# Two more chunk pairs of a projection as block products, and the recurrence's chunks ahead of them

## The chip, the core and the metric

The kernel runs on one core of a Trainium2 chip. The metric is device time in microseconds (us): the median of three runs. The core has a matrix engine (TensorE, PE in the profile; PEld is its loading of weights), a vector engine (VectorE, DVE), an engine for functions of one operand (ScalarE, ACT), GpSimd (POOL) and SyncE (SP). The last two issue transfers here: SyncE loads and stores, GpSimd transfers that add to what stands at their destination.

## The reference

One layer for x of 1024 positions by 1024 channels, all in float32:

```python
h = rms_norm(x, g_mix)
z = h @ w_in + b_in                       # 1024 -> 8 groups of columns
va, ga, xb, gb, sa, sb = split(z)         # 1024, 1024, 1536, 1536, 1024, 1024
u = conv31(va * sigmoid(ga))              # causal, per channel, 31 taps
y_a = silu(layer_norm(u)) @ w_a_out
v = rg_lru(conv4(xb))                     # 16 heads' gates, then a scan over positions
y_b = (v * gelu(gb)) @ w_b_out
x = x + (sigmoid(sa) * y_a + sigmoid(sb) * y_b) @ w_o
x = x + relu(rms_norm(x, g_mlp) @ w_1) ** 2 @ w_2
out = rms_norm(x, g_final)
```

The layer norm's mean and variance run over the 1024 channels of a position, so they need all eight convolutions.

## The kernel before

Positions are kept as two halves of 512, the even and the odd ones. A float32 operand is split into a high part that the fast matmul format holds and a low rest, and a product is three matmuls: high by high, high by low, low by high. One matmul is 128 by 128 weights against 512 positions.

The columns of w_in are taken in chunks of 128. VA and GA have 8 chunks each (j = 0 to 7), XB 12, GB 12, SA 8, SB 8.

*Part 1* (the loop over `s`, `chunk_mm`, L735) takes a chunk directly: 48 matmuls (8 blocks of 128 channels, 3 products, 2 halves). In before these are 28 chunks: all of XB, VA and GA, in the order of the list `CH`. Each chunk's weights are loaded (win_raw), written by ScalarE rounded and negated into the place of the low part (L66: win_l) and rounded into the high part (L68: win_h), and a GpSimd transfer adds the exact weights to the negated ones, so that the rest is left (L67). Behind a pair VA, GA, `u_out` forms u = va * sigmoid(ga): ScalarE at L587, VectorE at L453, a helper that records many of VectorE's operations. Between the chunks stand the gates of the recurrence: 16 heads (`head_mm`, L530 to L532), placed by the table `HS0`; behind every four heads (one group) come exponentials and roots on ScalarE (L556, L557, L564) and three scans on VectorE (`scan_tile`, L573 to L576, one for each of 12 tiles of 128 channels; its result is stored to hd). A scan is placed `lag` chunks late.

*Part 2* (the list `zseq`, `z_mm`, L933) takes two chunks together. Their weights are a matrix of 2 by 2 blocks (512 channels by 128 columns) and x is one of 2 by 2 blocks (512 channels by 512 positions). Seven products of blocks give the result that eight would (Strassen's way, in Winograd's form), of 12 matmuls each: 84 for a pair instead of 96. Product 1 and 2 and 4 use blocks of weights as they are; 3, 5, 6 and 7 use sums of blocks, made by VectorE (`z_sums`: zs). Each product's weights are split like the others (`z_lhs`: zo, from zw or zs), with the rest by a GpSimd transfer (L67), or for products 5 and 7 by ScalarE (L776) and VectorE (L453). Likewise products 4 to 7 use sums of x's blocks (`x_load` loads them as xs, `x_sum` adds, four per half of the positions, and `x_parts` splits them into xs4h, xs4l to xs7h, xs7l). A pair's weights are loaded by `z_load` in two halves (zw), in order of the table `ZL`. The results are put together out of the banks z..a to z..u by `z_out`. In before part 2 has 14 pairs: GB 6, SA 4, SB 4.

The convolutions (`conv`, L639 to L655) are VectorE's filling: eight of 49 operations, mostly taps (L648), which `vector_work` puts wherever VectorE would have to wait for TensorE by the planner's clocks (`at` adds an operation's assumed cost to an engine's clock; `later` holds an operation back until its operands are ready). `vector_work(inf)` in stage b takes whatever is left. Conv j's result is stored to yd[j] (L656), and `sum_up` has GpSimd add it into one tile ysum (L607, L609), with a transfer that accumulates.

*Stage b* multiplies by w_b_out (`b_mm`, L1121: eight steps j of 72 matmuls, banks yb). Its operand, the products of the scans and the gates, comes back from memory (hgd to hg) and is split: ScalarE (hgh, L1023), VectorE (hgl), twelve tiles, the last one behind stage b's first matmuls. Its weights are split by ScalarE (L1099) and VectorE (L1085). During step j = 1 the sum of the convolutions is split too (`n_parts`: ysumh by ScalarE, L1159; ysuml by VectorE), and at j = 2, behind 32 matmuls, `n_mean` places the four matmuls that give the mean (mu, L1149, L1150). The convolutions are loaded back as q by 16 loads (L1142), and the variance follows at j = 4. Behind that come the rest of the layer norm, w_a_out, w_o and the two products of the MLP, which the change leaves alone.

The order on each engine is the order in which the program states the operations (a manual schedule); nothing is reordered later. What the planner's clocks decide is only where VectorE's operations stand.

## Time and profile before

| | us |
|---|---|
| median of three runs | 1548.71 (1548.26 to 1549.64) |
| profiled execution | 1549.04 |
| its span | 1547.2 |
| PE, DVE, ACT, POOL busy | 1535.6, 1214.5, 903.6, 188.6 |
| part 2 begins (first matmul of z0a) | 360.57 |
| stage b begins (first matmul of yb) | 623.05 |
| mean's first matmul (mu) | 668.72 |

The lines of the profile read as: line of the kernel, engine, operation, written tile <- read tiles, shape, count, busy time, mean of one in ns, idle time before it and what ended that. In a timeline the first two numbers are start and duration in us, and in square brackets stand the idle time before it and its releaser. In a table of windows each engine has its busy us and its number of instructions, then the granted clock of TensorE (1.00 is full), the share of time in which the DMA engines were busy, and GB/s. Matmuls overlap by a little, so their durations (0.39) are longer than the spacing of their starts.

### The profile page before, as it was taken

How to read it: one execution, taken by the hardware profiler on the slowest of the kernel's cores; microseconds unless marked ns; L12 is line 12 of the kernel's file. 1: busy time of each engine (PE TensorE's matmuls, PEld its weight loads, DVE VectorE, ACT ScalarE, POOL GpSimd, SP SyncE). 2: the span in 40 equal slices, each digit the busy share in tenths (PEclk: the TensorE clock that was granted, in tenths of full speed). 3: DMA queues.
4: the chain of work that ended last, by engine and by line, in shares of the span. 5: the costliest groups of instructions: out<-in, count | busy, mean ns of one | idle time of the engine just before them, and what ended most of it. 6: DMA issues, size and time to landing. Idle time of an engine off the chain costs nothing. (4 is left out here: it accounts for less than half of the span.)

```text
span 1547.2 us, 19086 instructions
## 1 busy us (share of the span) xinstructions
PE 1535.6 (99%) x6804; PEld 1264.6 (82%) x6804; DVE 1214.5 (78%) x1641; ACT 903.6 (58%) x1266; POOL 188.6 (12%) x226
## 2 busy tenths in 40 slices
PE   9999999999999999999999999999999999999998
PEld 7878888788888888888888887888888888888886
DVE  6999989999899983468568868765555558888897
ACT  6748677576667667435375777545444475555553
POOL 0000000002222222000022322000000001111110
PEclk9999999999999999999999999999999999999999
DMA  8653554678999889854579978523333779888852
GB/s 348 169 127 95 160 140 134 158 227 214 264 267 256 195 206 259 270 196 126 185 195 306 194 171 198 211 75 124 113 115 111 242 216 229 226 223 223 205 124 109
DMA packets 124943, 294.18 MB, mean 190 GB/s; under 512 B 12464, under 2 KB 30512, under 8 KB 124848
## 3 DMA queue, kind: packets, MB, share of 16 engines
q1 hardware_dynamic: 93312, 213.00, 40.7%
q0 software_dynamic: 31392, 79.71, 28.1%
q8 instruction: 53, 0.87, 0.2%
q14 instruction: 42, 0.34, 0.1%
q10 hardware_dynamic: 144, 0.26, 0.1%
HBM read 152.93 MB, written 58.72 MB: 137 GB/s over the span
## 5 line engine op out<-in xcount | busy, mean ns | idle before, releaser
L735 PE MATMUL z<-xh,win_h 128*128 128x512 f32 x400 | 125.0, 390 | 0.0
L735 PE MATMUL z<-xl,win_h 128*128 128x512 f32 x400 | 123.5, 390 | 0.0
L1873 DVE TENSOR_TENSOR acc<-acc,d 128x1024 f32<-128x1024 f32 x72 | 87.8, 1220 | 33.4 <-PE d L1861 32.7
L735 PE MATMUL z<-xh,win_l 128*128 128x512 f32 x400 | 99.4, 391 | 0.0
L735 PEld LDWEIGHTS z<-xh,win_l 128*128 128x128 f32 x400 | 75.2, 188 | 16.8
L735 PEld LDWEIGHTS z<-xh,win_h 128*128 128x128 f32 x400 | 75.1, 188 | 16.5 <-ACT win_h L68 0.4
L648 DVE SCALAR_TENSOR_TENSOR y<-u,vec,y 128x511 f32<-128x511 f32 (+14 forms) x120 | 88.5, 737 | 0.0
L735 PEld LDWEIGHTS z<-xl,win_h 128*128 128x128 f32 x400 | 75.1, 188 | 15.8
L648 DVE SCALAR_TENSOR_TENSOR yt<-u,vec,yt 128x511 f32<-128x511 f32 (+6 forms) x112 | 82.6, 737 | 0.0
L648 DVE SCALAR_TENSOR_TENSOR y<-yt,csum,y 128x511 f32<-128x511 f32 (+6 forms) x112 | 82.6, 737 | 0.0
L542 ACT ACTIVATE g<-rg,vec 96x1024 f32<-96x1024 f32 x32 | 35.6, 1113 | 79.6 <-PE rg L532 79.6
L1540 ACT ACTIVATE o<-s 128x512 fp32r<-128x512 f32 x58 | 34.7, 623 | 52.8 <-DVE s L1525 31.3
L67 POOL DMA_DIRECT2D win_l<-win_raw x25 | 21.6, 865 | 319.1 <-ACT win_l L66 248.4
L476 DVE SCALAR_TENSOR_TENSOR v<-xb,vec,v 128x1023 f32<-128x1023 f32 (+2 forms) x36 | 46.2, 1282 | 11.4 <-ACT v L467 10.4
L67 POOL DMA_DIRECT2D zo<-zw x42 | 36.2, 862 | 133.6 <-ACT zo L66 125.3
L1121 PE MATMUL yb<-hgl,wb_h 128*128 128x512 f32 x168 | 51.8, 390 | 0.0
L1121 PE MATMUL yb<-hgh,wb_h 128*128 128x512 f32 x168 | 51.8, 389 | 0.0
L66 ACT ACTIVATE zo<-zw 128x512 fp32r<-128x512 f32 x42 | 26.3, 626 | 30.7 <-DMA zw<-in_w_in_dram 8.7
L67 POOL DMA_DIRECT2D db_1l<-wr x7 | 6.0, 860 | 309.8 <-DMA wr<-in_w_dram 254.0
L1121 PE MATMUL yb<-hgh,wb_l 128*128 128x512 f32 x168 | 41.0, 390 | 0.0
L1085 DVE TENSOR_TENSOR o<-s,o 128x512 fp32r<-128x512 f32 x58 | 38.8, 682 | 0.0
L1121 PEld LDWEIGHTS yb<-hgh,wb_h 128*128 128x128 f32 x168 | 31.6, 188 | 6.5
(1795 smaller groups left out, 4672.9 us busy)
## 6 DMA issues: line engine op xcount, KB each, us to landing
w_raw<-in_w_dram SPq DMA_DIRECT2D x36, 512.0 KB, 5.5
fr<-fd SPq DMA_DIRECT2D x32, 512.0 KB, 5.9
wr<-in_w_dram SPq DMA_DIRECT2D x32, 512.0 KB, 6.5
zw<-in_w_in_dram SPq DMA_DIRECT2D x28, 512.0 KB, 5.9
win_raw<-in_w_in_dram SPq DMA_DIRECT2D x25, 512.0 KB, 4.1
win_l<-win_raw POOLq DMA_DIRECT2D x25, 512.0 KB, 4.5
zo<-zw POOLq DMA_DIRECT2D x42, 256.0 KB, 5.6
gates<-zg SPq DMA_DIRECT2D x32, 256.0 KB, 4.0
```

The costliest lines, as they stand in the source:

```text
L66: nc.scalar.activation(l, src, AF.Copy, scale=-1.0)
L67: nc.gpsimd.dma_start(l, src, accum_op=ALU.add)
L476: nc.vector.scalar_tensor_tensor(v[:, d:S], a[:, 0:S - d], cbw_c[:, w * 12 + t:w * 12 + t + 1], v[:, d:S], ALU.mult, ALU.add)
L542: nc.scalar.activation(a, gps.pop((n, gi))[:HD, :], AF.Sigmoid, bias=(ba_c, bx_c)[gi][:, n:n + 1])
L648: nc.vector.scalar_tensor_tensor(o[:, k:], a[:, 0:HS - k], c, o[:, k:], ALU.mult, add)
L735: nc.tensor.matmul(zps[s][:, HALVES[hf]], w[:, k, :], xw[k][part][hf], start=n == 0, stop=n == 23)
L1085: tt(l, src, h.bitcast(F32), ALU.subtract)
L1121: nc.tensor.matmul(ps[hf], a, b[:, HALVES[hf]], start=n == 0, stop=n == len(todo) - 1)
L1540: nc.scalar.activation(o[:, 0], src, AF.Copy)
L1873: tt(acc[p, q2], acc[p, q2], ps, ALU.add)
```

## The change

VA and GA of j = 6 and 7 leave part 1 and become the first two pairs of part 2, which are now 16; a pair is VA j with GA j, and the new `z_branch` forms u out of the quadrants as they come. Part 1 has 24 chunks, in a new order: XB's chunks stand ahead of the VA, GA pair that they stood behind, and the heads follow (`HS0`). `lag` is 0 for all groups; tile 10's scan moves from part 1 to the start of part 2 (`ZX` slot 0), tile 11's from slot 7 to slot 2. `x_load` stands at the chunks 4 and 2 from the end, in place of 5 and 3, and several `x_parts` move into part 2.

In part 2 the first eight products are 1 and 2 of pairs 0 and 1 and then of pairs 2 and 3, with the rest of pairs 0 and 1 behind. The blocks that products 1 and 2 of pairs 2 and 3 need are loaded on their own (`z_first`: zf, four loads of 256 KB, before part 2), and their full loads come later as for the others. The loop over `z_sums` ahead of part 2 is gone; all are made within the loop. Of the four dummy matmuls that opened a bank (`z_bank`) one is left.

```diff
--- before.py
+++ after.py
@@ -668,7 +668,7 @@
 
     def x_load(c2):
 
-        xq[c2] = {n: ep.tile([P, S], F32, tag="e", name=f"xs{n}_{c2}") if (n, c2) == (21, 0) else T(f"xs{n}_{c2}")
+        xq[c2] = {n: ep.tile([P, S], F32, tag="e", name=f"xs{n}_{c2}") if (n, c2) == (22, 0) else T(f"xs{n}_{c2}")
                   for n in (11, 12, 22, 21)}
         for n, a in xq[c2].items():
             nc.sync.dma_start(a, xu[n % 10 - 1, 2 * (n // 10 - 1) + c2])
@@ -691,10 +691,8 @@
                 later(at("A", 1.0), 1.2, nc.vector.tensor_tensor, l, src, h.bitcast(F32),
                       ALU.subtract)
 
-    CH = [XB, VA, GA, XB + 1, XB + 2]
-    for js, g in (((1,), 1), ((2,), 2), ((3,), 3), ((4, 5, 6, 7), 4)):
-        CH += [c for j in js for c in (VA + j, GA + j)]
-        CH += [XB + t for t in range(3 * g, min(3 * g + 3, 12))]
+    NJ = 6
+    CH = [XB + 0, VA + 0, GA + 0, XB + 1, XB + 2, XB + 3, XB + 4, XB + 5, VA + 1, GA + 1, XB + 6, XB + 7, XB + 8, VA + 2, GA + 2, XB + 9, XB + 10, XB + 11, VA + 3, GA + 3, VA + 4, GA + 4, VA + 5, GA + 5]
     NC1 = len(CH)
     zps = {n: z0[n] for n in range(N0)}
     wraw, wst = {}, {}
@@ -736,8 +734,8 @@
                                  start=n == 0, stop=n == 23)
         at("P", len(halves) * (n1 - n0) * MM)
 
-    ZPAIRS = [GB + 2 * i for i in range(6)] + [SA + 2 * i for i in range(4)]
-    ZPAIRS += [SB + 2 * i for i in range(4)]
+    ZPAIRS = [(VA + j, GA + j) for j in range(NJ, 8)]
+    ZPAIRS += [(c, c + 1) for c in range(GB, SB + 8, 2)]
     NZ = len(ZPAIRS)
     zraw, zs, zo, zb = {}, {}, {}, {}
     zn = [0]
@@ -745,8 +743,14 @@
     def z_load(i, kk):
 
         zraw[i, kk] = raw = qp.tile([P, 2, 4, P], F32, tag="p", name=f"zw{i}_{kk}", bufs=4)
-        c = ZPAIRS[i]
-        nc.sync.dma_start(raw, w_in[c:c + 2, :, 4 * kk:4 * kk + 4, :].rearrange("m p k c -> p m k c"))
+        c, d = ZPAIRS[i]
+        nc.sync.dma_start(raw, w_in[c:d + 1:d - c, :, 4 * kk:4 * kk + 4, :].rearrange("m p k c -> p m k c"))
+
+    def z_first(i):
+        for kk in range(2):
+            zraw[i, 0, kk] = raw = sp_.tile([P, HS], F32, tag="s", name=f"zf{i}_{kk}").rearrange(
+                "p (k c) -> p k c", c=P)
+            nc.sync.dma_start(raw, w_in[ZPAIRS[i][0], :, 4 * kk:4 * kk + 4, :])
 
     def z_blk(i, m_, kk):
         return zraw[i, kk][:, m_]
@@ -767,8 +771,11 @@
             S_(4, z_blk(i, 0, 1), zs[i, 2], ALU.subtract)
 
     def z_lhs(i, p):
-        src = z_blk(i, *{1: (0, 0), 2: (0, 1), 4: (1, 1)}[p]) if p in (1, 2, 4) else \
-            zs[i, {3: 4, 5: 1, 6: 2, 7: 3}[p]]
+        if p in (1, 2) and 2 <= i < FIRST:
+            src = zraw[i, 0, p - 1]
+        else:
+            src = z_blk(i, *{1: (0, 0), 2: (0, 1), 4: (1, 1)}[p]) if p in (1, 2, 4) else \
+                zs[i, {3: 4, 5: 1, 6: 2, 7: 3}[p]]
         zn[0] += 1
         o = (wp.tile([P, 2, 4, P], F32R, tag="w", name=f"zo{i}_{p}") if zn[0] % 5 > 2 or zn[0] % 5 == 0 else
              qp.tile([P, 2, 4, P], F32R, tag="g", name=f"zo{i}_{p}", bufs=2))
@@ -782,29 +789,32 @@
         zo[i, p] = o
 
 
-    zseq = [(0, 1), (1, 1), (0, 2), (1, 2), (0, 6), (0, 7), (1, 7), (0, 5), (1, 6), (0, 3), (0, 4),
-            (1, 5)]
+    FIRST = 4
+    zseq = [(i, p) for g in ((0, 1), (2, 3)) for p in (1, 2) for i in g]
+    zseq += [(0, 6), (0, 7), (1, 7), (0, 5), (1, 6), (0, 3), (0, 4), (1, 5)]
     for i in range(2, NZ):
-        zseq += [(i, 1), (i, 7), (i - 1, 4), (i, 6), (i, 2), (i - 1, 3), (i, 5)]
+        zseq += [x for x in ((i, 1), (i, 7), (i - 1, 4), (i, 6), (i, 2), (i - 1, 3), (i, 5))
+                 if x not in zseq]
     zseq[-7:] = [(NZ - 1, p) for p in (1, 7, 6)] + [(NZ - 2, 4), (NZ - 1, 2), (NZ - 1, 5), (NZ - 2, 3)]
     zseq += [(NZ - 1, 3), (NZ - 1, 4)]
 
     ZL = {}
     for i in range(2, NZ):
-        n = zseq.index((i, 1))
-        ZL[n - 9] = ((z_load, i, 0),)
-        ZL[n - (6 if i > 2 else 4)] = ((z_load, i, 1),)
+        n = zseq.index((i, 7)) - 1
+        a, b = {2: (8, 4), 3: (10, 6)}.get(i, (9, 6))
+        ZL[n - a] = ((z_load, i, 0),)
+        ZL[n - b] = ((z_load, i, 1),)
     def z_get(n, f):
         return f(*zseq[n]) if 0 <= n < len(zseq) else None
 
     ENGINES = {mybir.EngineType.Activation, mybir.EngineType.DVE, mybir.EngineType.PE,
                mybir.EngineType.SP, mybir.EngineType.Pool}
-    HS0 = [4 + 5 * (n // 4) + n % 4 for n in range(NH)]
+    HS0 = [(4, 8, 12, 17)[n // 4] + n % 4 for n in range(NH)]
     head_at = {s: n for n, s in enumerate(HS0)}
 
     EXP = {head_slot: g for g, head_slot in enumerate(HS0[4 * g + 3] + 1 for g in range(4))}
-    XL = {23: 0, 25: 1}
-    XS = {25: ((x_parts, 0, 6),), 26: ((x_parts, 0, 7, 5),), 27: ((x_parts, 0, 4),)}
+    XL = {NC1 - 4: 0, NC1 - 2: 1}
+    XS = {NC1 - 1: ((x_parts, 0, 6),)}
     w_load(3)
     head_w(0)
     w_load(4)
@@ -865,7 +875,7 @@
             for d in range(6):
                 if s - d in EXP:
                     g = EXP[s - d]
-                    lag = int(g < 3)
+                    lag = 0
                     if d == 0:
                         scan_exp(g)
                         scan_in(begun + 3.5, 3 * g, 3 * g + 1)
@@ -875,7 +885,7 @@
                         scan_root(g)
 
                     t = 3 * g + d - 2 - lag
-                    if 3 * g <= t < 3 * g + 3 and t < 11:
+                    if 3 * g <= t < 3 * g + 3 and t < 10:
                         later(rooted[t], 4.8, scan_tile, t)
             if s == NC1 - 1:
                 z_get(0, z_lhs)
@@ -917,7 +927,7 @@
     hgd = dp.tile([12, P, S], F32, name="hgd")
     def z_bank(i, b):
         zb[i, b] = t = zp.tile([P, HS], F32, tag="z", name=f"z{i}{b}")
-        if i < 2 and b in "be":
+        if i == 0 and b == "b":
 
             nc.tensor.matmul(t, xh[0][0][:, 0:P], xh[0][0][:, 0:HS], start=True, stop=True)
         return t
@@ -936,9 +946,11 @@
         at("P", 12 * MM)
 
     def z_out(i, m_, hf, src, name):
-        ci = ZPAIRS[i] + m_
+        ci = ZPAIRS[i][m_]
         bias = bin_c[:, ci:ci + 1]
-        if ci < SA:
+        if ci < XB:
+            z_branch(ci, hf, src, bias)
+        elif ci < SA:
             t = ci - GB
             h = hb.pop((t, hf))
             a = src if name else EV(f"ze{i}{m_}{hf}")
@@ -957,11 +969,37 @@
             at("A", 0.62)
             nc.sync.dma_start(halved(spill[b, j], hf), g)
 
+    zu, zg = {}, {}
+
+    def z_branch(ci, hf, src, bias):
+        j = ci % GA
+        if j not in zu:
+            zu[j] = T(f"u{j}")
+        d, g = halved(zu[j], hf), src.rearrange("p (n o) -> p o n", o=2)
+        if ci >= GA:
+            zg[j, hf] = g
+            nc.scalar.activation(src, src, AF.Sigmoid, bias=bias)
+            ready = at("A", 0.62)
+            if hf == 0:
+                later(ready, 0.63, nc.vector.tensor_tensor, d, d, g, ALU.mult)
+                z_joined(j)
+        elif hf == 0:
+            nc.scalar.activation(d, g, AF.Identity, bias=bias)
+            at("A", 0.62)
+        else:
+            later(0, 0.68, nc.vector.scalar_tensor_tensor, d, g, bias, zg.pop((j, hf)), ALU.add, ALU.mult)
+            z_joined(j)
+
+    def z_joined(j):
+        if j in ut:
+            fresh.append(j)
+        ut[j] = zu[j]
+
     hb = {}
 
     def z_h(i, m_, hf):
-        t = ZPAIRS[i] + m_ - GB
-        if t < 12:
+        t = ZPAIRS[i][m_] - GB
+        if 0 <= t < 12:
             hb[t, hf] = h = EV(f"hb{t}_{hf}")
             nc.sync.dma_start(h, hd[t, :, HALVES[hf]])
 
@@ -994,7 +1032,9 @@
         elif p == 4:
             z_out(i, 1, 0, zb[i, "u"], "c")
 
-    ZX = {0: ((x_parts, 1, 7),), 7: ((later, 0, 4.8, scan_tile, 11),), 2: ((x_parts, 1, 5),), 4: ((x_parts, 1, 4),)}
+    ZX = {0: ((x_parts, 1, 6), (later, 0, 4.8, scan_tile, 10)), 2: ((x_parts, 0, 7), (later, 0, 4.8, scan_tile, 11)),
+          3: ((x_parts, 1, 7),), 6: ((x_parts, 0, 5),), 7: ((x_parts, 1, 5),), 9: ((x_parts, 0, 4),),
+          10: ((x_parts, 1, 4),)}
     H_AT = {2: (0, 0), 5: (1, 1), 3: (0, 1), 4: (1, 0)}
     with tc.manual_schedule(engines=ENGINES):
 
@@ -1032,13 +1072,12 @@
                    L - 4: ((hg_parts, 5, 6), (hg_load, 7)), L - 3: ((hg_load, 8, 9),),
                    L - 2: ((hg_parts, 7, 8), (hg_load, 10)), L - 1: ((hg_load, 11),),
                    L: ((hg_parts, 9, 10),), L + 1: ((hg_parts, 11),)})
-        for n in range(6):
-            z_get(n, z_sums)
+        z_first(2)
+        z_first(3)
         vector_work(clk["V"])
         z_get(2, z_lhs)
         z_get(3, z_lhs)
-        u_out(7, zps[NC1 - 2], zps[NC1 - 1])
-        x_parts(1, 6)
+        u_out(NJ - 1, zps[NC1 - 2], zps[NC1 - 1])
         vector_work(clk["V"])
         z_h(0, 0, 0)
         for n in range(len(zseq) + 2):
@@ -1059,8 +1098,7 @@
                     z_h(i, *H_AT[p])
             z_get(n, z_mm)
             z_get(n + 4, z_lhs)
-            if n > 0:
-                z_get(n + 5, z_sums)
+            z_get(n + 5, z_sums)
             if n < L:
                 for f, *a in ZX.get(n, ()):
                     f(*a)
```

## The prediction

> **What bounds the kernel now.** I read the page first (busy shares, PE's waits, transfers), then windows around the two places that the change touches, then the timeline there, row by row.
>
> ```profile
> span 1547.2 us, 19086 instructions
> PE 1535.6 (99%) x6804; PEld 1264.6 (82%) x6804; DVE 1214.5 (78%) x1641; ACT 903.6 (58%) x1266; POOL 188.6 (12%) x226
> ```
> ```profile
> PE gu4a L1297 <- ACT u_late L1351: 1.6, 1, 1.6
> PE z4e L933 <- DMA zo<-zs: 0.2, 1, 0.2
> ```
> ```profile
> 350.00:400.00 50.00, 50.00 (x222) 41.42 (x221) 47.63 (x68) 33.89 (x55) 12.01 (x14) 1.00 0.87 225
> ...
> 550.00:600.00 50.00, 50.00 (x222) 41.41 (x222) 31.59 (x49) 30.20 (x54) 11.26 (x13) 1.00 0.91 209
> ```
>
> TensorE (PE) works 1535.6 of 1547.2 us, at clock 1.00, and waits for almost nothing behind the start: 1.6 us once, in a late stage, and 0.2 us for one block product's weights. So the time is the number of matmuls times their spacing, plus any wait that the change creates. VectorE (DVE) is nearly full early in part 2 (47.63 of 50 us) and has slack from 550 us on (31.59); there the convolution finishes.
>
> **The gain: 27 matmuls fewer.** Spacing comes from 23 rows of two matmuls each in stage b, without a pause:
>
> ```profile
> 645.14 0.62 PE L1121 MATMUL yb<-hgh,wb_h 128*128 128x512 f32 x2
> ...
> 655.57 0.62 PE L1121 MATMUL yb<-hgl,wb_h 128*128 128x512 f32 x2
> ```
>
> 655.57 − 645.14 = 10.43 us over 46 matmuls: 0.2267 each. Four chunks leave part 1 (4 × 48 = 192), two pairs enter part 2 (2 × 7 × 12 = 168), and of four dummy matmuls that open a bank one is left: −192 + 168 − 3 = −27, times 0.2267 = **−6.1 us**. All are on PE's path, so this counts in full. Without a new wait: 1549.04 − 6.1 = 1542.9 in the profiled execution, 1542.6 beside the median (1548.71 is 0.33 under the profiled run; I subtract that from each time below).
>
> **Wait A: the first product of sums.** What the diff moves: the gate scans of tiles 10 and 11 (tile 11 was in part 2 before, but later), and the sums of x for the second half come one chunk closer to the border between the parts. The rows of before:
>
> ```profile
> 314.26 0.74 DVE L648 SCALAR_TENSOR_TENSOR y<-yt,csum,y 128x500 f32<-128x500 f32 x1
> 314.91 0.74 DVE L648 SCALAR_TENSOR_TENSOR yt<-u,vec,yt 128x500 f32<-128x500 f32 x1
> ...
> 316.74 0.62 PE L735 MATMUL z<-xh,win_h 128*128 128x512 f32 x2
> 325.86 1.28 DVE L453 SCALAR_TENSOR_TENSOR u<-z,vec,u 128x1024 f32<-128x1024 f32 x1 [1.35 <-ACT u L587]
> 327.06 4.99 DVE L453 TENSOR_TENSOR xs<-xs,xs 128x1024 f32<-128x1024 f32 x4
> 331.97 1.22 DVE L573 SCALAR_TENSOR_TENSOR g<-a,g 128x1024 f32<-128x1024 f32 x1
> 332.02 1.90 SPq L674 DMA_DIRECT2D xs<-xu  x4
> 333.97 2.83 SPq L749 DMA_DIRECT2D zw<-in_w_in_dram  x4
> 336.82 0.53 DVE L641 TENSOR_SCALAR y<-yt,csum,cab 128x512 f32<-128x512 f32 x1
> 337.92 1.22 DVE L453 TENSOR_TENSOR xs6l<-xs,xs6h 128x1024 fp32r<-128x1024 f32 x1
> 360.57 0.39 PE L933 MATMUL z0a<-xh,zo 128*128 128x512 f32 x1
> ...
> 363.47 0.62 ACT L66 ACTIVATE zo<-zs 128x512 fp32r<-128x512 f32 x1
> 364.52 0.87 POOL L67 DMA_DIRECT2D zo<-zs  x1 [2.25 <-ACT zo L66]
> 371.90 0.39 PE L933 MATMUL z0b<-xs6h,zo 128*128 128x512 f32 x1
> ```
> ```profile
> zo<-zw POOLq DMA_DIRECT2D x42, 256.0 KB, 5.6
> zo<-zs POOLq DMA_DIRECT2D x28, 256.0 KB, 6.9
> hb<-hd SPq DMA_DIRECT2D x24, 256.0 KB, 6.3
> ```
>
> Let T be the first matmul of part 2 (360.57 before; 192 × 0.2267 = 43.5 earlier after). Before, the transfer that splits product 6's weights was issued 3.95 us behind T (364.52); with 6.9 it lands at 371.4 by the median, and the first matmul that needs it (the third, 372.36) did not wait: about 1 us to spare. After, product (0,6) is ninth instead of fifth, because four products of pairs 2 and 3 go first. Its third matmul is due at T + 8 × 12 × 0.2267 + 0.45 = **T + 22.2**.
>
> DVE's queue in front of it, in order. The u of chunk pair 4 starts at chunk start + 9.12 (325.86 − 316.74), that is T − 21.8 + 9.1 = T − 12.6, and takes 1.2. Six taps at 0.65 (314.91 − 314.26), 3.9: T − 7.5. Scan 9 takes 336.82 − 331.97 = 4.85: T − 2.7. Four sums of x 4.9 (331.97 − 327.06): T + 2.2. xs6l and u5, 1.2 each: T + 4.6. Scan 10: T + 9.5. xs6l of the other half: T + 10.7. Scan 11: T + 15.5. xs7l: T + 16.7. Two weight sums, as wide as a tap, at 0.65: T + 18.0. Then ScalarE copies (0.62) and GpSimd's transfer starts 1.05 behind the copy's start (364.52 − 363.47): T + 19.1. With 6.9 us it lands at **T + 26.0**: PE waits 3.8. The fastest and the slowest transfer of this tile give the ends:
>
> ```profile
> DMA to landing us min/median/max: 3.3/6.1/9.4
> ```
>
> T + 22.4 to T + 28.5, so 0.2 to 6.3; were DVE 4 us quicker than the sum, 0. I take **3.8**, the median of its own kind. The later products behind it (0,7), (1,7), (0,5) are due 2.7 us apart and their sums are ready in that order, so I cost them at nothing.
>
> The new loads of pairs 2 and 3 (four of 256 KB) stand on SyncE's queue behind the store of scan 9, so they start about T − 2.3. The first is needed at product (2,1), fifth: third matmul T + 11.3, less 1.05 and 5.6: landed by T + 4.6, which leaves 6.9 us. The row nearest in size, hb from memory, has 6.3: no wait, but only just (second rival).
>
> **Wait B: the mean of the convolution.** In part 1 fewer taps fit, so the convolution ends later. In DVE's order before, its last tap is ahead of all hg splits; after, 18 taps and three closing adds of conv 7 stand behind the last hg split (hgl11) and two splits of w_b_out. The chain from there to the mean's matmul (mu), with the rows of before:
>
> ```profile
> 575.50 0.69 DVE L655 TENSOR_TENSOR y<-y,yt 128x511 f32<-128x511 f32 x1
> 623.05 0.62 PE L1121 MATMUL yb<-hgh,wb0h 128*128 128x512 f32 x2
> 637.79 1.23 DVE L453 TENSOR_TENSOR hgl<-hg,hgh 128x1024 fp32r<-128x1024 f32 x1 [2.45 <-ACT hgh L1023]
> 639.18 1.83 DVE L1085 TENSOR_TENSOR wb_l<-wb_raw,wb_h 128x768 fp32r<-128x768 f32 x2 [0.16 <-ACT wb_h L1099]
> 645.12 1.29 DVE L1128 TENSOR_TENSOR sb<-yb,sb 128x512 f32<-128x512 f32 x2 [4.11 <-PE yb L1121]
> 649.30 1.04 ACT L1159 ACTIVATE ysumh<-ysum 128x1024 fp32r<-128x1024 f32 x1
> 650.38 1.22 DVE L1085 TENSOR_TENSOR ysuml<-ysum,ysumh 128x1024 fp32r<-128x1024 f32 x1 [0.19 <-ACT ysumh L1159]
> 651.88 11.16 SPq L1142 DMA_DIRECT2D q<-yd  x16
> 668.96 0.40 PE L1150 MATMUL mu<-ysuml,onesr 128*128 128x512 f32 x1
> ```
> ```profile
> yd<-y SPq DMA_DIRECT2D x8, 512.0 KB, 4.0
> ysum<-yd POOLq DMA_DIRECT2D x8, 512.0 KB, 8.7
> ```
>
> Let Y be stage b's first matmul (623.05). Before, the conv was done at 576.2 and mu had everything at 651.6, 17 us early. mu's second matmul stands 668.96 − 623.05 = 45.9 behind Y, and as many matmuls lie between in both kernels. After: hgl11 and the splits end at Y + 18.0 (641.0); 15 taps 9.8 → 27.8; two sb products 1.3 → 29.1; two splits 1.9 → 31.0; three taps 2.0 → 33.0; three adds 2.0 → 35.0; the store 4.0 → 39.0; GpSimd's accumulate 8.7 → 47.7; ScalarE 1.1, DVE 1.2 → **Y + 50.0**: PE waits **4.1**. The eight stores and the eight accumulates of before have these ends:
>
> ```profile
> DMA to landing us min/median/max: 2.6/4.0/8.7
> ```
> ```profile
> DMA to landing us min/median/max: 6.1/8.7/9.6
> ```
>
> A store at 2.6 and an accumulate at 6.1 give Y + 46.0, no wait; 8.7 and 9.6 give Y + 55.6, 9.7. The 16 loads of q wait on SyncE behind this same store; they run beside the accumulate now. The Trainium skill (DMA: Bandwidth & Descriptors, section "Issuing engines are not separate DMA queues") says that transfers run on the same 16 DMA engines and interleave, whichever engine issued them; by that rule the accumulate would be slower than its row, and the wait at the upper end. No run here shows the two together. Who is queued behind: SyncE reaches the q loads at Y + 35 (658.0) instead of 651.88, and the weight loads of j = 4 behind them as much later, about Y + 46, for a use 4 × 72 matmuls behind Y (Y + 65): free.
>
> **Costed at nothing.** The second pairs' extra copies, bank reads and stores (ScalarE's 33.89 of 50 and GpSimd's 12.01 have room; if ScalarE had none, each late copy would cost PE its 0.62); the four zf loads' bytes, which pairs 2 and 3 load a second time (1 MB, at 225 GB/s 4.7 us of the transfers, in a stretch where PE waits for none but those of A); DVE's eight more weight sums and the sigmoid products, 217 taps and some 208 others between u5 and hgl11, at 0.65 to 0.7 about 283 us, for 1345 matmuls (305) less 4.6 plus 14.7, 315: no steady shortage.
>
> **Sum.** 1549.04 − 6.1 + 3.8 + 4.1 = 1550.8 profiled, **1550.4** beside the median.
>
> **Rivals.**
> *One wait only.* Only B, because six taps are all that A's sum has to shed: −6.1 + 4.1, 1546.7. Only A, because the store and the accumulate fall to their quick ends: 1546.4. For: the rows' spread. Against: both chains are longer than their due times at the medians.
> *No wait:* 1542.6. For: before, such transfers cost PE 0.2 us in all. Against: the same two sums.
> *Slower: the new loads come late.* The first four zw loads before were issued together with the xs loads (332.02 and 333.97) and those loads stand side by side here too, just in front of the zf loads. If zf needs over 6.9 us, PE waits at (2,1). The slowest of the zw loads of before shows how far that can go:
>
> ```profile
> DMA to landing us min/median/max: 3.3/5.6/21.1
> ```
>
> At 21.1 the wait is 14.2; at half the way 7.1. ScalarE's copy for xs6l stands behind the late load, so A shrinks by only a part (I take 2): 1550.4 + 7.1 − 2 = 1555.5. For: issuing took 2.83 us for four there, where a queue was full. Against: 256 KB, not 512, and the median 5.6.
> *The clock falls behind a wait.* The granted clock is 1.00 in both windows above, and no wait behind the start is longer than gu4a's 1.6. Were the clock at half behind a 3.8 us wait for as long as the wait was, 3.8 / 0.4534 = 8.4 matmuls would take 0.2267 more each, 1.9 per wait: 1552.3 with one such wait, 1554.2 with both. For: nothing here. Against: the waits are short. The Trainium skill (TensorE: Matmul & The Clock Gate, "HAM oscillation — how this bites in real kernels") says that a pause over about 3.4 us brings the clock to half until it is warm again, and both my waits are about that long; no trace here has such a pause. By its figure the price would be 1.7 instead of 1.9, an estimate from that page.
>
> **How the numbers follow.** Both waits, without the clock: 0.37, its own range 1546 to 1555. Only one: 0.25. None: 0.10. Late loads: 0.15. Clock: 0.13. 0.2% (3.1 us) is about what a measurement of this kernel can tell from no change: faster is under 1545.6, slower over 1551.8. Faster: none 0.10, half of "one" 0.10, a tail of both 0.04: 0.24. Slower: loads 0.15, clock 0.09, the upper part of both 0.13: 0.37. The rest, 0.39, is the same. The range goes from just under the one-wait cases to the late loads, with a tenth left out on each side: 1543.5 to 1557.
>
> **What the changed profile would show.** The gain: some 6749 PE matmuls in the program, part 2 starting about 43.5 us earlier, stage b about 5.5. Wait A: PE idle before z0b, released by the transfer zo<-zs, none before z2a; wrong if z0b follows z3a at once or if z2a waits. Wait B: PE idle before mu, released by ysumh or ysuml, with the last accumulate landing around Y + 48. Wrong altogether if PE waits in the middle of part 2, which I hold to be free.

## The result and the profile after

The changed kernel takes 1568.69 us (median; 1567.81 to 1569.82), 1.0129 times the kernel before, with a 95% interval of 1.0112 to 1.0147. That is 20.2 us slower than the four runs of before that were timed beside it (median 1548.49; the 1548.71 above is the median of three of them). Forecast were 1550.4, with a range up to 1557.0. The profiled execution took 1569.27 us with a span of 1567.5, 20.3 more than before.

Busy times hardly differ: the page of the changed kernel shows PE at work for 1536.3 us against 1535.6, with 27 matmuls fewer (6777 for 6804).

```profile
span 1567.5 us, 19111 instructions
...
PE 1536.3 (98%) x6777; PEld 1261.2 (80%) x6777; DVE 1224.5 (78%) x1659; ACT 916.6 (58%) x1295; POOL 194.2 (12%) x232
```

So the matmuls are gone, and the time came from outside them. The view of PE's waits (us in total, times, longest) names where; before, only two entries stood behind the start.

```profile
PE rg L530 <- ACT g L542: 5.8, 5, 2.1
PE mu L1187 <- ACT ysumh L1197: 4.0, 1, 4.0
PE z1f L943 <- DVE zc L453: 2.7, 1, 2.7
PE z2a L943 <- ACT z2b L1009: 2.6, 1, 2.6
PE gu4a L1335 <- ACT u_late L1389: 2.1, 1, 2.1
PE z15e L943 <- ACT zc L1020: 2.0, 1, 2.0
...
PE z4a L943 <- DMA zo<-zw: 1.4, 1, 1.4
...
PE mu L1188 <- DVE ysuml L1123: 0.5, 1, 0.5
```

Heads in part 1 5.8, four places in part 2 8.7 (2.6, 2.7, 1.4, 2.0), the mean 4.5: 19.0 us of waits that the kernel before did not have. gu4a's wait is 0.5 longer than before, the start's two are 0.2 longer together, and the 0.2 of z4e is gone: 0.5 more. The sum, 19.5, agrees with the page: span less PE's busy time was 11.6 and is 31.2.

PE's busy time is 0.7 longer although 6.1 us of matmuls are gone, so the matmuls that are left take 6.8 us more. Windows cut at the places where the granted clock (the number behind the counts) changes show it:

```profile
257.50:260.90 3.40, 1.26 (x6) 0.67 (x5) 3.36 (x3) 3.40 (x5) 0.70 (x1) 1.00 0.71 135
260.94:264.35 3.41, 3.41 (x10) 2.48 (x9) 3.28 (x4) 2.11 (x4) 0.00 (x0) 0.50 0.11 19
377.00:380.41 3.41, 2.88 (x7) 2.30 (x8) 3.41 (x6) 1.25 (x2) 0.00 (x0) 0.50 0.34 88
684.20:691.02 6.82, 4.98 (x11) 3.60 (x12) 5.46 (x8) 3.20 (x5) 0.00 (x0) 0.50 1.03 367
691.02:694.40 3.38, 3.38 (x17) 2.77 (x16) 3.28 (x6) 2.06 (x4) 0.00 (x0) 1.00 1.01 344
```

Three stretches at half clock, 3.41 + 3.41 + 6.82 = 13.64 us, and each stands behind a wait (the second head wait at 260, z1f, the mean). At half clock half of the work time is lost: 6.8 us at most, and 5.6 by PE's busy time in these stretches, which hold some of the waits. The account, with the 6.8 of PE's busy time as a whole: −6.1 + 19.5 + 6.8 = 20.2, against 20.3 measured. Part 2 begins 35.3 us earlier than before (43.5 were forecast), stage b 10.7 us later (5.5 earlier were forecast).

The rows that answer to those of wait A, in the changed kernel's timeline (T, the first matmul of z0a, is at 325.30):

```profile
342.19 0.69 DVE L453 TENSOR_TENSOR zs<-zs,zw 128x512 f32<-128x512 f32 x1
342.91 0.63 ACT L66 ACTIVATE zo<-zs 128x512 fp32r<-128x512 f32 x1 [4.77 <-DVE zs L453]
343.84 0.86 POOL L67 DMA_DIRECT2D zo<-zs  x1 [6.29 <-ACT zo L66]
343.97 0.58 ACT L1009 ACTIVATE z2b<-z2a 128x512 f32<-128x512 f32 x1
344.60 0.50 PE L943 MATMUL z2a<-xh,zo 128*128 128x512 f32 x1 [2.59 <-ACT z2b L1009]
350.17 0.39 PE L943 MATMUL z0b<-xs6h,zo 128*128 128x512 f32 x1
```

VectorE's second weight sum ends at T + 17.6 (forecast T + 18.0), the transfer starts at T + 18.5 (19.1). But the matmul that waits is another: product 2 of pair 2 writes on in bank z2a, which ScalarE first copies to z2b, and that copy (343.97) stands in ScalarE's queue behind the copy of the late sum (342.91, which waited 4.77 us). It cost 2.6, two products earlier than I looked. The transfer itself landed after 4.0 us, not 6.9:

```profile
zo<-zs POOLq DMA_DIRECT2D x1, 256.0 KB, 4.0
```

So the weights of (0,6) were there at T + 22.5, by the sum 0.3 behind their due time, and z0b itself, 2.6 later by then, did not wait. VectorE's rows stand in the forecast order, close to the forecast times; that a wait of 2.6 stands beside a forecast of 3.8 is luck, as another instruction waited, for another reason.

Wait B, with stage b's first matmul (Y) at 633.79:

```profile
654.26 0.74 DVE L648 SCALAR_TENSOR_TENSOR yt<-u,vec,yt 128x503 f32<-128x503 f32 x1
...
670.36 0.68 DVE L655 TENSOR_TENSOR y<-y,yt 128x511 f32<-128x511 f32 x1
685.56 1.22 DVE L1123 TENSOR_TENSOR ysuml<-ysum,ysumh 128x1024 fp32r<-128x1024 f32 x1 [14.52 <-ACT ysumh L1197]
```
```profile
674.56 0.87 POOL L609 DMA_DIRECT2D ysum<-yd  x1 [40.56 <-DMA yd<-y]
```
```profile
685.58 0.79 PE L1187 MATMUL mu<-ysumh,onesr 128*128 128x512 f32 x1 [4.02 <-ACT ysumh L1197]
686.84 0.80 PE L1188 MATMUL mu<-ysuml,onesr 128*128 128x512 f32 x1 [0.46 <-DVE ysuml L1123]
```

This is the forecast chain in order: the last add ends at Y + 37.3 (35.0), the accumulate starts 3.5 later (4.0), ScalarE's copy follows 9.9 after that, at 684.47 (8.7), and PE waits 4.5 (4.1). The closeness of the last pair is partly luck: the chain as a whole ends 3.0 later than forecast (Y + 53.0 for Y + 50.0), and PE came to the mean 2.1 late itself, mostly by the 2.0 that it had waited at z15e.

### The profile page after: what moved, and what is told of

The parts are those of the page before. It is cut to its first block, busy times and chain, and to the rows that moved or that the text cites. A ratio compares the mean times of both kernels' runs of the same rounds, so it can differ in the third digit from the quotient of the medians.

```text
span 1567.5 us, 19111 instructions
## 1 busy us (share of the span) xinstructions
PE 1536.3 (98%) x6777; PEld 1261.2 (80%) x6777; DVE 1224.5 (78%) x1659; ACT 916.6 (58%) x1295; POOL 194.2 (12%) x232
## 4 chain that ended last, share of the span: by engine, by line
PE 84%; DMA 6%; ACT 5%; DVE 3%; issue 2%; SPq 0%; POOL 0%; DVEq 0%; ACTq 0%; POOLq 0%
PE d L1899 15%; PE z L733 10%; PE yb L1159 6%; PE e L2016 3%; PE keep L1899 2%; PE z L258 2%; DMA hg<-hgd 1%; PE rg L530 1%; PE rg L532 1%; PE rg L531 1%; DVE y L648 1%; DMA zo<-zw 1%; DMA w_raw<-in_w_dram 1%; ACT a L556 1%; DMA ysum<-yd 1%
## 5 line engine op out<-in xcount | busy, mean ns | idle before, releaser
L733 PE MATMUL z<-xh,win_h 128*128 128x512 f32 x336 | 105.6, 392 | 0.0
L733 PE MATMUL z<-xl,win_h 128*128 128x512 f32 x336 | 104.1, 391 | 0.0
L648 DVE SCALAR_TENSOR_TENSOR y<-u,vec,y 128x511 f32<-128x511 f32 (+14 forms) x120 | 88.8, 740 | 0.0
L733 PE MATMUL z<-xh,win_l 128*128 128x512 f32 x336 | 84.1, 391 | 0.0
L648 DVE SCALAR_TENSOR_TENSOR yt<-u,vec,yt 128x511 f32<-128x511 f32 (+6 forms) x112 | 83.0, 741 | 0.0
L648 DVE SCALAR_TENSOR_TENSOR y<-yt,csum,y 128x511 f32<-128x511 f32 (+6 forms) x112 | 83.0, 741 | 0.0
L542 ACT ACTIVATE g<-rg,vec 96x1024 f32<-96x1024 f32 x32 | 35.6, 1113 | 80.6 <-PE rg L532 80.6
L733 PEld LDWEIGHTS z<-xh,win_h 128*128 128x128 f32 x336 | 63.5, 189 | 14.3 <-ACT win_h L68 0.4
L733 PEld LDWEIGHTS z<-xh,win_l 128*128 128x128 f32 x336 | 63.1, 188 | 14.3
L733 PEld LDWEIGHTS z<-xl,win_h 128*128 128x128 f32 x336 | 63.4, 189 | 13.4
L67 POOL DMA_DIRECT2D win_l<-win_raw x21 | 18.2, 867 | 294.7 <-ACT win_l L66 213.9
```

The source lines that it names most:

```text
L67: nc.gpsimd.dma_start(l, src, accum_op=ALU.add)
L542: nc.scalar.activation(a, gps.pop((n, gi))[:HD, :], AF.Sigmoid, bias=(ba_c, bx_c)[gi][:, n:n + 1])
L648: nc.vector.scalar_tensor_tensor(o[:, k:], a[:, 0:HS - k], c, o[:, k:], ALU.mult, add)
L733: nc.tensor.matmul(zps[s][:, HALVES[hf]], w[:, k, :], xw[k][part][hf], start=n == 0, stop=n == 23)
```

## The experiments

All are made from the changed kernel or, where it is said, from a version with one pair. "Now" is 1568.69; the kernel before took 1547.97 to 1548.20 beside these runs.

**The half clock: work put in the place of a wait.**

```diff
         ps = bank(name)
+        if name == "mu0":
+            for _ in range(20):
+                nc.tensor.matmul(ps, hg[0][0][:, 0:P], hg[0][0][:, 0:HS], start=True, stop=True)
         nc.tensor.matmul(ps, onesr, h, start=True, stop=False)
```

> The changed kernel, with 20 matmuls (4.5 us) whose result is not used in front of the mean's, in the place of the wait. They change nothing that is computed. Theory (a wait of TensorE brings its clock to half for some us): the wait is filled, the clock stays at full, and 3.4 us are won although 20 matmuls were added: about 1565.3. Rival (the half clock comes from something else, such as power or the transfers): the same time as the changed kernel, 1568.7, half clock still there.

Measured: 1565.76 (1.0111 times before, 1.0096 to 1.0126), 2.9 us less than now. The difference in time is small (the slowest run here took 1567.68, the fastest of the changed kernel 1567.81); the clock in the trace is clear. The timeline and a window of this run:

```profile
682.18 4.69 PE L1189 MATMUL mu<-hgh 128*128 128x512 f32 x20
```
```profile
687.40:690.80 3.40, 2.70 (x12) 2.25 (x13) 3.40 (x5) 0.85 (x2) 0.00 (x0) 1.00 1.06 383
```

The clock is 1.00 where it was 0.50. The transfers went on as before (the DMA engines' share is 1.06 here and 1.03 there), so the half clock belongs to the wait and not to them.

**The mean's wait taken away.**

```diff
-            if j == 2 and n == 16:
+            if j == 2 and n == 28:
                 n_mean()
+            if j == 4 and n == 12:
+                n_var(0)
+                n_var(1)
...
-            if j == 4:
-                n_var(0)
-                n_var(1)
```

> The changed kernel, with the mean's matmuls 24 matmuls (5.4 us) later in step j = 2 and the variance's 24 later in step j = 4. Theory: the wait of 4.0 + 0.5 us goes, and with it the 6.8 us of half clock behind it (worth 3.4): 7.9 us less, about 1561. Rival A (the half clock has nothing to do with the wait): 4.5 less, about 1564. Rival B (the mean's lateness is only handed on): TensorE waits for the variance instead, no change.

Measured: 1563.49 (1.0099, 1.0082 to 1.0116), 5.2 less instead of 7.9. In the profile the wait of mu is gone, nothing waits for the variance, and the stretch behind it is at full clock, so rival B falls. Part of what is missing, 1.7, came back elsewhere: behind z2a, whose wait is unchanged (2.62), the clock fell in this run, as it did not in the changed kernel's:

```profile
340.70:344.10 3.40, 0.87 (x4) 0.74 (x5) 3.22 (x6) 2.40 (x5) 0.86 (x1) 1.00 0.76 225
344.20:347.60 3.40, 3.40 (x9) 2.63 (x9) 2.77 (x5) 3.38 (x5) 0.88 (x1) 0.51 0.94 214
```

Nothing in the program ahead of that place differs. The traces show what does. Within one trace the stretches at half clock start whole multiples of 3.413 us apart (in the changed kernel at 260.95, 377.00 and 684.20, that is 34.0 and 90.0 times; it is so, to within 0.02 of a multiple, in all ten traces that have two or more). The clock thus falls only on a grid of 3.413 us, which lies elsewhere in each execution. In the changed kernel z2a's wait falls on two windows of its grid:

```profile
339.45:342.86 3.41, 2.56 (x12) 1.78 (x10) 3.38 (x5) 0.00 (x0) 0.00 (x0) 1.00 0.49 162
342.86:346.28 3.42, 1.68 (x7) 1.42 (x8) 3.24 (x6) 3.21 (x7) 0.86 (x1) 1.00 0.82 197
```

PE is idle there for 0.85 and 1.74 us, and the clock stays; in this run one window holds 2.53 of the wait (3.40 less 0.87), and the next is at half clock. Cut on their grids, the thirteen traces with such a stretch (the changed kernel's and twelve of these runs') have 28 windows at full clock with 1.96 us or more idle: half clock followed each. Under 1.5 us it followed none, and of the 20 windows between it followed six. So whether a wait of 1.5 to 3.9 us costs 1.7 more is partly a matter of where it falls, and not of the program alone.

**Tile 11's scan later.**

```diff
-2: ((x_parts, 0, 7), (later, 0, 4.8, scan_tile, 11)),
+2: ((x_parts, 0, 7),),
...
-7: ((x_parts, 1, 5),),
+7: ((x_parts, 1, 5), (later, 0, 4.8, scan_tile, 11)),
```

> The changed kernel, with tile 11's scan put back from slot 2 to slot 7 of part 2. Theory (the chain of VectorE in front of the first weight sums is too long by this scan, 4.85 us): the 2.59 us wait of z2a goes, because ScalarE no longer stands at the copy of that sum in front of bank z2b: 2.6 us less, about 1566. Rival: VectorE is as full behind, so the 4.85 us come out again at z1f (now 2.71 us): no change, or up to 2 us slower.

Measured: 1568.90 (1.0132, 1.0117 to 1.0147), no change. z2a waits no more, so VectorE's chain is the cause of that wait, and z1f takes it all back:

```profile
PE z1f L943 <- DVE zc L453: 7.2, 1, 7.2
```

From 2.7 to 7.2, close to the scan's 4.85. The rival's outcome came: what one place is spared the next one pays. Its reason, that VectorE has too much work there, is not the whole of it, as the next run shows.

**Why z1f waits.** Two rows of the changed kernel's timeline stand ahead of z1f's releaser:

```profile
358.10 0.86 POOL L67 DMA_DIRECT2D zo<-zw  x1 [0.60 <-ACT zo L66]
```
```profile
367.86 0.69 DVE L453 TENSOR_TENSOR zs<-zw,zw 128x512 f32<-128x512 f32 x1 [4.69 <-DMA zw<-in_w_in_dram]
```

VectorE idles for 4.69 us for the second half of pair 2's weights, with bank z1f's sum (zc) in its queue behind. By the program that load goes into the buffer that the transfer at 358.10 (product (0,4)) still reads, and the view of SyncE's waits from 350 to 372 us has 9.8 us in front of a load of weights (L747) for such a transfer (zo from zw). The run has (2,6), which needs these weights, one product later:

```diff
+    a, b = zseq.index((2, 6)), zseq.index((1, 3))
+    zseq[a], zseq[b] = zseq[b], zseq[a]
     zseq[-7:] = [(NZ - 1, p) for p in (1, 7, 6)] + ...
```

> The changed kernel, with product (2,6) and product (1,3) exchanged, so that the sums that need the late second half of pair 2's weights are due one product (2.7 us) later. Theory (VectorE's 4.7 us wait for these weights at 363 makes it late for bank z1f): the wait of 2.71 at z1f and the half clock behind it (1.7) go: 4.4 less, about 1564. Rival (VectorE is late there by its amount of work, as the run with the later scan showed): no change.

Measured: 1567.02 (1.0123, 1.0108 to 1.0138), 1.7 less; its four runs lie between 1564.94 and 1569.06 and overlap those of now, so the time alone shows no gain. The trace does at this place: VectorE's wait for the weights is gone,

```profile
368.22 0.69 DVE L453 TENSOR_TENSOR zs<-zw,zw 128x512 f32<-128x512 f32 x1 [0.19 <-DMA zw<-in_w_in_dram]
```

z1f's wait falls from 2.7 to 1.2, and the half clock at 377 is gone. A half clock at 636 (behind z15e, where the wait is as before) and waits of 1.0 at z1a and 0.7 at z2e came up. So the late weights are a cause of z1f's wait, of some 1.5 us of it and of the half clock behind it; the rest stays.

**Part 2 begun as before.**

```diff
-    FIRST = 4
-    zseq = [(i, p) for g in ((0, 1), (2, 3)) for p in (1, 2) for i in g]
+    FIRST = 2
+    zseq = [(i, p) for p in (1, 2) for i in (0, 1)]
...
-        z_first(2)
-        z_first(3)
+        z_get(4, z_sums)
```

(with the splits of x's sums in earlier slots, as this order needs them)

> The changed kernel, without the early products of pairs 2 and 3: part 2 begins with products 1 and 2 of two pairs, as before, and product (0,6) is fifth. Theory (the chain of VectorE ends at about 25 us behind the border): z0b is due at 11.3 and waits about 14 us, the wait of z2a (2.6) and those of z1f (2.7 and 1.7 of half clock) go: about 7 us slower, 1576. Rival (the early products cost VectorE and the transfers as much as they win): no change.

Measured: 1576.87 (1.0182, 1.0167 to 1.0197), 8.2 slower than now, 7 expected. Taking the products of four pairs first, with the loads and slots that belong to it, is worth that much here. The mechanism was not as told: the waits are 2.3 at z0a, 2.0 at z1f and 4.4 at z0e, with 6.8 us of half clock among them, not 14 at z0b. That the totals agree is luck.

**The filler of VectorE.** In part 1 the changed order gives VectorE less to do. The windows from 100 to 350 us (after, part 2 begins at 325.30, and no tap stands between there and 350), of VectorE's taps alone (L648), before and then after:

```profile
100.00:350.00 250.00, 94.39 (x142) 1.00 0.58 152
```
```profile
100.00:350.00 250.00, 59.41 (x89) 0.99 0.61 160
```

53 taps fewer. The run puts one pair back:

```diff
-XB + 2, XB + 3, XB + 4, XB + 5, VA + 1, GA + 1, XB + 6,
+XB + 2, VA + 1, GA + 1, XB + 3, XB + 4, XB + 5, XB + 6,
...
-    HS0 = [(4, 8, 12, 17)[n // 4] + n % 4 for n in range(NH)]
+    HS0 = [(4, 9, 13, 17)[n // 4] + n % 4 for n in range(NH)]
```

> The changed kernel, with only the pair VA 1, GA 1 put back ahead of XB 3 to 5, and the second and third head groups one chunk later (first heads at 4, 9, 13, 17). Theory (part 1 gives VectorE too few taps, because the u they need come late): 13 operations fewer of the convolution stand behind the last hg split, 8.5 us; the mean's wait of 4.5 us goes and the half clock behind it (3.4); the wait of 0.60 at the first head border goes; the border between the third and fourth group loses its gap and costs 1 to 4 more than now. Together about 1560 to 1562. Rival (the taps only move; VectorE falls behind in part 2 instead): no change.

Measured: 1564.52 (1.0101, 1.0084 to 1.0118), 4.2 less. The mean no longer waits and its half clock is gone, as told. By 350 us only 6 taps more were done than in the changed kernel (95 for 89), so that it isn't their number there alone that decides; the run moves two groups of heads as well, and does not separate the two. And z1f lost much of the gain again:

```profile
PE z1f L943 <- DVE zc L453: 7.7, 1, 7.7
```
```profile
350.00:400.00 50.00, 42.26 (x175) 34.34 (x173) 34.09 (x52) 29.22 (x48) 10.03 (x12) 0.90 0.69 164
```

VectorE waits there and is not full (34.09 of 50): 6.27 us for the same half of pair 2's weights and 5.18 us for a transfer that still reads a sum of weights (zo from zs). With the products exchanged and (0,4) ahead of (0,3), so that the buffer comes free earlier:

```diff
-    zseq += [(0, 6), (0, 7), (1, 7), (0, 5), (1, 6), (0, 3), (0, 4), (1, 5)]
+    zseq += [(0, 6), (0, 7), (1, 7), (0, 5), (1, 6), (0, 4), (0, 3), (1, 5)]
```

> The changed kernel with VA 1, GA 1 early (as in the run with only that), and with products (2,6) and (1,3) exchanged and (0,4) ahead of (0,3). Theory (z1f waits because the load of the second half of pair 2's weights waits for the buffer that product (0,4)'s transfer still reads, and VectorE for the load): VectorE's wait of 6.3 us shrinks by 5.4, z1f's wait from 7.7 to 2 or less, the 10.2 us of half clock behind it (5.1) go: about 1553 to 1555. Rival (VectorE has too much work there in any order): 1562 or more.

Measured: 1559.99 (1.0068, 1.0051 to 1.0085), 8.7 less than now. VectorE no longer waits for these weights, but still 3.48 us for that transfer from zs; z1f waits 2.8 and the half clock there is 6.8 us instead of 10.2. The direction is right; some 5 us of the gain did not come, of which 1.7 are a half clock behind a head's wait of 1.73 at 142.

**The heads in part 1.** The two largest waits of PE for a gate, and ScalarE's rows ahead of them:

```profile
248.43 2.96 ACT L564 ACTIVATE g<-g 128x1024 f32<-128x1024 f32 x3
251.41 1.28 ACT L542 ACT_TABLE_LOAD   x1
252.70 1.11 ACT L542 ACTIVATE g<-rg,vec 96x1024 f32<-96x1024 f32 x1
...
257.90 0.80 ACT L630 ACTIVATE y<-u,vec 128x512 f32<-128x512 f32 x1
258.60 0.71 ACT L631 ACTIVATE yt<-u,vec 128x512 f32<-128x512 f32 x1
259.21 1.10 ACT L542 ACTIVATE g<-rg,vec 96x1024 f32<-96x1024 f32 x1
```
```profile
253.87 0.48 PE L530 MATMUL rg<-vth,rgh 96*96 96x512 f32 x1 [1.66 <-ACT g L542]
...
260.36 0.47 PE L530 MATMUL rg<-vth,rgh 96*96 96x512 f32 x1 [2.13 <-ACT g L542]
```

A gate waits behind the roots of the group before, a table load, and then the copies of weights (two rows of 1.05, left out above) and a convolution's first operations. All heads share one bank, so PE cannot go on to the next head's half. Two runs were aimed at this. The first moves the gate forward in ScalarE's queue:

```diff
+            if before is not None:
+                head_gate(before, 1, clk["P"] - 12 * MM)
             w_parts(s + 1)
             if s == 3 or c >= XB:
                 vector_work(0)
-            if before is not None:
-                head_gate(before, 1, clk["P"] - 12 * MM)
```

> The changed kernel, with each head's second gate on ScalarE put ahead of the next chunk's weight copies. Theory (ScalarE's queue is too full at the borders of head groups): the two waits of TensorE for that second gate (0.81 us at 190, 2.13 us at 260) go, and the half clock that follows the second one (3.4 us, worth 1.7) goes too; the three waits for the first gates (0.60, 0.61, 1.66) stay. Together 4.6 us less, about 1564. Rival (ScalarE is short of time in these chunks as a whole): the weights of the next chunk come late instead and TensorE waits there, no change or slower.

Measured: 1585.04 (1.0231, 1.0216 to 1.0247), 16 slower than now. The gates' waits grew from 5.8 to 7.1, PE waited for weights (win_h 1.5, win_l 0.9), the mean's wait became 9.5 and half clock 27 us. The rival's outcome came, and more. That ScalarE is short of time in these chunks as a whole is not shown, though. It works 121.04 us of the 170 from 100 to 270 in the changed kernel, and less in this run (the fourth pair of numbers is ScalarE's):

```profile
100.00:270.00 170.00, 161.74 (x688) 127.17 (x687) 125.08 (x141) 119.59 (x121) 10.32 (x12) 0.98 0.49 120
```

Only around the last border, from 247 to 262, is it nearly full in the changed kernel (14.42 of 15). The edit moved the gate of all sixteen heads, and ScalarE's own waits for a head's matmuls in front of a gate grew from 80.6 to 86.2 us, the longest from 7.4 to 8.4: what stands in the queue behind a gate that must wait comes later too. That this made the weights late is argued from these numbers, not shown by a run.

The second moves a group of heads by one chunk (`(4, 8, 13, 17)`):

> The changed kernel, with the third head group one chunk later (13 to 16), so that the gap that lay between the third and the fourth group lies between the second and the third. Theory (TensorE waits where the exponentials or roots of one group and the gates of the next are in the same chunks): the waits at 185 and 190 (1.4 together) go or shrink, and the waits at the border of the last groups, 3.8 now, stay or grow, with about 1.4 there for the exponentials. No change within 2 us in all. Rival (the waits belong to the place, not to the gap): the two waits at 185 and 190 stay.

Measured: 1568.48 (1.0133, 1.0119 to 1.0147), no change. The waits at 185 and 190 became one of 1.60 at 197, and those at the last border stayed, 0.60 and 2.12. It told little: the waits follow the group (they moved by a chunk), but their total hardly changed, 4.9 for 5.8, so that the missing gap alone makes them is not shown. No run gives back the roots' lag alone, so which part of the new order makes the 5.8 us stays open.

**One pair instead of two, in the order of before.** Chunks, heads, lag and first products as before, 26 direct chunks, one pair (VA 7, GA 7) by block products:

```diff
-    NJ = 6
+    NJ = 7
...
+    for js, g in (((1,), 1), ((2,), 2), ((3,), 3), ((4, 5, 6), 4)):
...
-    HS0 = [(4, 8, 12, 17)[n // 4] + n % 4 for n in range(NH)]
+    HS0 = [4 + 5 * (n // 4) + n % 4 for n in range(NH)]
...
-                    lag = 0
+                    lag = int(g < 3)
```

> Only one pair (VA 7, GA 7) taken by block products, with the order of chunks, the heads, the lag of the scans and the order of products of the kernel before; tiles 10 and 11 are scanned in slots 5 and 7. Theory (the waits come from the new order and from too much work at the border, not from the block products themselves): 15 matmuls fewer, 3.4 us, no wait of the mean: about 1545. Rival (any pair more at the border makes VectorE late there): waits of TensorE in the first 20 products of 3 to 6 us, about 1548 to 1551.

Measured: 1558.98 (1.0068, 1.0053 to 1.0083). No head waits and the mean doesn't, as the theory said; but the border does:

```profile
PE z0a L946 <- DVE u L453: 7.1, 1, 7.1
PE z L736 <- ACT win_h L68: 2.8, 1, 2.8
```

The time is above the rival's too. With the old order and one pair the waits in part 1 and at the mean are gone; the run changes the order, the lag and the number of pairs together, and for the mean the run with VA 1, GA 1 early shows that two pairs can do without the wait as well. The border of the parts has trouble of its own. Three more runs followed that. ScalarE relieved in the last chunks (x's sums split a chunk later) and the banks of the last chunks turned by one:

```diff
+            if s == 22:
+                PS("zskip")
...
-    XS = {NC1 - 3: ((x_parts, 0, 6),), NC1 - 2: ((x_parts, 0, 7, 5),), NC1 - 1: ((x_parts, 0, 4),)}
+    XS = {NC1 - 2: ((x_parts, 0, 6),), NC1 - 1: ((x_parts, 0, 7, 5),)}
```

> The kernel with one pair more by block products, as in the run before it, but with less on ScalarE in the last chunks (the copy of x's sums for products 6 one chunk later, those for 7 and 5 in the last chunk, that for 4 in part 2) and with the banks of the last chunks turned by one, so that the first bank of part 2 isn't one that the last u still reads. Theory: the waits at the last chunk (2.8 us), at z0a (7.1) and the half clock behind it (3.4) go: 13.3 less, about 1546, faster than the kernel before. Rival: the splits of the first products then come late by their transfers, waits of 2 to 4 us at the first four products, 1549 to 1551.

Measured: 1559.07 (1.0067, 1.0052 to 1.0082): the wait for win_h went, z0a's 6.1 and its half clock stayed, since the first bank was still the last VA chunk's. With the last pair as GA, VA and its sigmoid a chunk earlier, and the banks not turned any more:

```diff
-            if s == 22:
-                PS("zskip")
...
+    CH[-2:] = [GA + 6, VA + 6]
...
-        u_out(NJ - 1, zps[NC1 - 2], zps[NC1 - 1])
+        u_out(NJ - 1, zps[NC1 - 1], None)
```

> The one-pair kernel of the last run, with the last direct pair taken in the order GA, VA and its sigmoid placed behind the GA chunk. Theory (z0a waits because its bank still holds a chunk that the last u reads on VectorE): the bank is free one chunk earlier, the wait of 6.06 us and its half clock (3.4) go: 9.5 less, about 1549.5; no faster than before by more than 1, because four small waits of part 2 (3.5 us together) eat the 3.4 us of the 15 matmuls. Rival (ScalarE and VectorE are late there anyway): another wait of 3 to 6 us at the first four products.

Measured: 1551.77 (1.0021, 1.0012 to 1.0030), 7.3 less than the run before it and with no half clock between the start and the end. The waits that are left are small, and all belong to the border and to transfers:

```profile
PE z0f L952 <- DVE zc L453: 1.6, 1, 1.6
...
PE z0a L952 <- DMA zo<-zw: 1.5, 2, 1.2
...
PE z2e L952 <- DMA zo<-zs: 0.7, 1, 0.7
PE z0a L952 <- ACT z0b L1018: 0.6, 1, 0.6
```

With the scans of tiles 10 and 11 in slots 6 and 10:

> The same, with the scans of tiles 10 and 11 in slots 6 and 10 instead of 5 and 7. Theory: VectorE is less full up to the fifth product, the wait at z0f (1.1) goes, about 1548.5. Rival: it moves on, no change.

Measured: 1552.50 (1.0031, 1.0021 to 1.0041). z0f's wait went; waits of 2.1 at z0a and 1.1 at z2a and 6.8 us of half clock came in the profiled execution, which was the slowest of the nine (1556.49). No version of these beats the kernel before; the nearest is 0.2% slower.

## Why the prediction was wrong

Forecast was the same time within the measurement, and it came 20 us slower. The gain and the two waits that were in the sum came out near their sizes. The step that failed is what was costed at nothing or left out: waits in part 2 behind the first product of sums, waits of the heads in part 1, and the clock behind all of them.

**The gain** held. 27 matmuls fewer, and PE's part of the account is closed with −6.1 us. (6804 less 27 is the 6777 that the page shows; the 6749 of the forecast is a slip.)

**Wait A** held by its chain up to the sum (T + 17.6 for 18.0) and failed behind it. The transfer took 4.0 for 6.9, and the ready time was compared with z0b's due time alone, while ScalarE's queue held the bank copy for z2a behind the same sum. Forecast 3.8, measured 2.6 at z2a; "wrong if z0b follows z3a at once or if z2a waits" names just what came.

**Wait B** held: 4.1 forecast, 4.5 measured. Its terms came out as 37.3 for 35.0, 3.5 for 4.0, 9.9 for 8.7. The chain was 3.0 longer than forecast and PE 2.1 late itself, so that the two waits agree so closely is partly luck. The sentence of the Trainium skill (DMA: Bandwidth & Descriptors, "Issuing engines are not separate DMA queues"), that transfers share the DMA engines whichever engine issued them, would make the accumulate slower beside q's loads. It landed after 9.5 us, above the median of before (8.7) and inside its range (6.1 to 9.6), so this one transfer neither shows that nor excludes it.

**"The later products ... I cost them at nothing"** and "PE waits in the middle of part 2, which I hold to be free" failed: z1f (product (1,4)) 2.7, z4a 1.4, z15e 2.0, together 6.1. The count of VectorE's work over the whole of part 2 was right (283 of 315 us forecast, 286.5 of 322 measured) and answered another question: in the first 50 us VectorE waited 4.69 us for weights whose buffer I had not followed, and was late by that. At z15e ScalarE's copy stands behind splits of hg that wait for loads. No run was aimed at z15e or z4a.

**Part 1 was not in the sum at all.** "In part 1 fewer taps fit" was there only as the cause of B. The new places of the heads were listed and their effect on ScalarE, with one bank for all heads, was not worked out: 5.8 us.

**The clock** was a rival with a chance of 0.13 and a price of 1.9 for a wait. It was right as a mechanism, and with 19 us of waits in place of 7.9 it cost 6.8. I had written "For: nothing here". The Trainium skill's page (TensorE: Matmul & The Clock Gate, "HAM oscillation — how this bites in real kernels") speaks of pauses over about 3.4 us; the runs agree on the half clock and differ on the threshold: z1f's single wait of 2.71 sufficed, and so did one of 1.62 in the run with the later scan, while 2.6 at z2a did in one run and not in another. By these traces what decides is the idle time in one window of the grid: from 1.96 us on in every case, between 1.5 and 1.95 in some. The stretches measured were 3.41 us long, or 6.82 and 10.2 where PE was idle for 0.7 us or more in the first window at half clock as well.

The forecast of 1550.4 thus missed 5.8 of heads, 6.1 of later products, 6.8 of clock and 0.5 at other places, and had 0.8 too much for A and B: together 18.4, where 18.3 us lie between forecast and result.

## What to carry to other kernels

When TensorE works without a pause, count each new wait twice: its own length and, from some 1.5 us on, a possible stretch at half clock behind it (3.41 us here, 1.7 lost). A step that frees one engine's time moves other engines' work: ask for every engine, stretch by stretch and not over a whole stage, whether it still has its filling and its room, and for every late result which other instruction stands behind it in the same queue. Where a fix at one place gives its gain back at the next, look for what both places wait for, over the whole stretch.

## What was not expected

Twenty matmuls of no use in the place of a wait made a kernel 2.9 us faster. And the same program text gave half clock behind a 2.6 us wait in one kernel's profile and full clock in another's, because the clock is set on a grid of 3.413 us that lies elsewhere in each execution. So a profile of one execution may show one or two such stretches, 1.7 us each, more or fewer than the next.
